# Down-projection regrouped: 4 plain chunks and five Strassen groups with sums in DRAM, three products of a pair added in PSUM, a 48-row projection in widths 512 and 128

## The chip, the cores and the metric

The kernel runs on one core of a Trainium2 chip. The metric is the device time of one execution in microseconds. The engines are TensorE (PE in the profile, its weight loads PEld), VectorE (DVE), ScalarE (ACT), GpSimd (POOL) and SyncE (SP), which here only issues DMAs.

## The reference

One layer of a streaming encoder for 512 prompt frames and 8 x 16 sample frames, 640 token columns in all, with a model width of 2048: a modulated norm, one input projection (its 16 columns for decay and beta are the "48-row projection"), a gated delta rule and a windowed attention, an output projection, and the feed-forward part that the change is about:

```python
x = x + gate1 * (jnp.concatenate([o_d, o_a], axis=-1) @ w_o)
h2 = rms_norm(x, norm2_w) * (1 + scale2) + shift2
u = h2 @ w_up                        # 2048 -> 2 * 5632
u_ext = jnp.concatenate([ffn_prev, u], axis=1)
u_c = causal_dwconv(u_ext, ffn_conv_w) + ffn_conv_b
gt, up = jnp.split(u_c, 2, axis=-1)
x = x + gate2 * ((jax.nn.silu(gt) * up) @ w_down)      # 5632 -> 2048
```

## The kernel before

Activations lie with features on the 128 partitions and the 640 token columns along the free axis, in two halves of 320 (`HALF`): 16 feature chunks for the model width, 44 for the feed-forward width (`NFF`). Every matmul of these projections is done as three in fp32r, high weight by high token part, high by low, low by high. So each weight block of 128 x 512 (a "unit", four chunks) is split on the chip: ACT casts it (`whi`), DVE subtracts (`wlo`). Units come in a fixed stream that `build_stream` writes down; `next_unit` keeps four of them ahead of PE.

The up-projection and part of the down-projection use Strassen's seven products of a 2 x 2 block problem. A product needs a weight operand that is one block or the sum of two (`wsum`, on DVE or POOL), a token operand that is likewise one quarter or a sum of two (`msum`), split in two parts as well, and its result is combined with others afterwards. `product` issues one; `ORDER` = (2, 4, 5, 1, 6, 7, 3) is the order of the seven, each with a PSUM bank of its own.

In the up-projection (`up`, one call for each of 44 pairs) a product has 24 matmuls of 320 columns. Its results are combined into the rows that `conv` then convolves, gates and stores in DRAM (`md`).

The down-projection walks over the 44 chunks in groups, `DGRP` = ((0, 4), (1, 8), (0, 4), (1, 8), (0, 4), (1, 8), (0, 8)). A plain group (0, m) takes m chunks and all 16 output rows, six matmuls for each chunk and row. A split group (1, 8) takes 8 chunks; `down(f)` makes the rows f and f + 8 by seven products of 12 matmuls, 84 in all. `DPOOL` says that of the five weight sums those for products 5, 1 and 7 go to POOL. After each result, `resid` multiplies it by the gate and adds it to `y`, the residual stream, which stays in SBUF through all groups (loaded from `xd`): a scaled add of 256 columns and a product of 64 on DVE, an add of 64 on POOL. `mixes` makes the token operands (`mop`) of a split group from chunks (`mraw`), mostly during the plain group ahead of it; its transfers are issued by POOL.

The order of the instructions on each engine is fixed when the program is built: `Lane`s of background work are stepped between matmuls, as a small model of the engines' clocks permits.

`ab` projects the 16 decay and beta columns, high and low parts in 48 rows of the array, with 64 matmuls of 320 columns.

Of the kernel before, what the change touches and what calls it, by code (L numbers as in the profile page):

```python
# [16 lines left out]
ORDER = (2, 4, 5, 1, 6, 7, 3)  # L17
NF = 8
# [76 lines left out]
class Model:  # L95
    """Estimates when each engine and each tile is free, to order the instructions of parallel tasks."""
# [79 lines left out]
class Ring:  # L176
    """Slots taken in turn, each a tag of a pool."""
# [18 lines left out]
class Slots:  # L196
    """Tiles of any width up to n in the slots of a ring."""
# [30 lines left out]
class Kern:  # L228
# [80 lines left out]
    def build_stream(self):  # L309
# [23 lines left out]
        for i in range(NFF):  # L333
            quarters("u", i, ORDER[4:] if i < NP else ORDER, i < NP)
        n = 0
        for split, m in DGRP:
            for u in range(0 if split else 4 * m):
                self.add_unit(u % 2, (("d", n + u // 2), d["wdn"][n + u // 2]))
            for f in range(8 if split else 0):
                for p in ORDER:  # L340
# [54 lines left out]
    def mm_quarter(self, ps, unit, acts, first, last):  # L395
        nc = self.nc
        hi, lo = unit
        for k, (xh, xl) in enumerate(acts):
            for i, (w, x) in enumerate(((hi, xh), (hi, xl), (lo, xh))):
                nc.tensor.matmul(out=ps, lhsT=w[:, k, :], rhs=x, start=first and k == 0 and i == 0,  # L400
                                 stop=last and k == len(acts) - 1 and i == 2)
# [230 lines left out]
    def ab(self, pool, kp, st):  # L632
        nc, d = self.nc, self.d
        ps, pv = self.main_ps()
# [12 lines left out]
        ps_evac(nc, ps[0:48], a48[:, 0:512].rearrange("p (s c) -> p s c", s=2),  # L647
                a48[:, 512:640].rearrange("p (s b t) -> p s b t", s=2, t=TS))
# [803 lines left out]
    def mix_start(self):  # L1452
        """The last gate and the first block of the output projection, as their operands come."""
# [58 lines left out]
    def head(self, h):  # L1512
        """Convolved queries and keys of head h; calling the result gives them with the values."""
# [28 lines left out]
    def phase2(self):  # L1542
# [4 lines left out]
        self.md = tc.dram_tile([NFF, P, NT], F32, name="md")  # L1547
        self.pd = tc.dram_tile([NP, 4, P, HALF], F32, name="pd")
        with tc.tile_pool(name="xres", bufs=1, reuse_waits="tile") as xr, \
# [20 lines left out]
            with tc.tile_pool(name="opx", bufs=1, reuse_waits="tile") as ox:  # L1570
# [3 lines left out]
                with tc.tile_pool(name="ffn", bufs=1, reuse_waits="tile") as fp:  # L1574
                    self.ffn(Tiles(nc, fp, 1))

    def attn_out(self, pa, load):
        """Output projection with its residual, norm, and the first products of NP pairs."""
# [87 lines left out]
    def operand(self, p, j):  # L1666
        """Token operand of product p for the features of chunks j and j + 8, as a sum of two parts."""
# [34 lines left out]
    def pipe(self, ks, ops, s=0, rB=None):  # L1702
        """Steps that scale rows ks, then make the operands ops, a stage of it a step."""
# [45 lines left out]
    def product(self, p, step=None, nh=2):  # L1749
        ps = self.next_bank()  # L1750
        for h in range(nh):
            un = self.next_unit()
            self.feed(self.rate)
            for k in range(4):
                while len(self.ops[p]) <= 4 * h + k:
                    if self.bg:
                        self.feed()
                    else:
# [3 lines left out]
                self.mm_quarter(ps, (un[0][:, k:k + 1], un[1][:, k:k + 1]), [x], h == 0 and k == 0,  # L1762
                                h == nh - 1 and k == 3)
# [4 lines left out]
    def ffn(self, fp):  # L1768
# [17 lines left out]

        def up(i):
# [8 lines left out]
            e = hs[i] if i < NP else fp.tile([P, HALF], F32, tag="e", name="e")  # L1796
            for q, pr in enumerate(ORDER):
                if i < NP and q < 4:
                    continue
                ps = self.product(pr, lambda: mid(2 * q, t5))  # L1800
                if pr == 2:
                    nc.scalar.copy(out=t2, in_=ps)
                elif pr == 4:
                    p4 = ps
                elif pr == 5:
                    nc.scalar.copy(out=t5, in_=ps)
                    nc.gpsimd.tensor_tensor(out=e, in0=t2, in1=t5, op=ALU.add)
                elif pr == 1:
                    v.tensor_tensor(out=e, in0=ps, in1=e, op=ALU.subtract)
                    step(7)  # L1810
                    ext = [prep(i, n) for n in range(2)]
                    add(v, quad(ext[1], 0), qin(p4), qin(t2))
                elif pr == 6:
                    v.tensor_tensor(out=t2, in0=ps, in1=e, op=ALU.add)
                elif pr == 7:
                    v.tensor_tensor(out=e, in0=ps, in1=e, op=ALU.add)
                    if i < NP:
                        ext = list(short)
                    add(nc.gpsimd, quad(ext[0], 0), quad(ext[1], 0), qin(e))
                elif pr == 3:  # L1820
                    add(v, quad(ext[0], 1), qin(ps), qin(t5))
                    add(nc.gpsimd, quad(ext[1], 1), quad(ext[0], 1), qin(t2))
                step(2 * q + 1)
                if i == NFF - 1 and q == 3:
                    self.lanes["c"].add(chunks())
# [76 lines left out]
        acts, ops, raws, ap, ox = {}, {}, [], self.ap, self.ox  # L1902
        stag = [(ap, f"a{x}{k}") for k in range(6, 16) for x in "hl"] + [(ox, f"ex{k}") for k in range(8)]
        spare = Ring(None, "", 0)
        spare.slots = [[ap, f"a{x}{k}", None] for k in (4, 5) for x in "hl"]
        sums = Slots(spare, NT)

        def raw(c):
            tag = ("ftm", "fext")[len(raws) // 2 % 2]
            raws.append(c)  # L1910
            t = fp.tile([P, 658], F32, tag=tag, name="mraw", bufs=2)[:, 0:NT]
            nc.gpsimd.dma_start(out=t, in_=self.md[c])
            return t

        def whole(c, s, t):
            """Both parts of chunk c, in slot s."""
            tags = [(ap, f"a{x}{s}") for x in "hl"] if s < 4 else stag[2 * s - 8:2 * s - 6]
            hi, lo = (p.tile([P, NT], F32R, tag=n, name=f"m{x}") for x, (p, n) in zip("hl", tags))
            yield (t,)
            nc.scalar.copy(out=hi, in_=t)  # L1920
            yield (hi,)
            v.tensor_tensor(out=lo, in0=t, in1=hi.bitcast(F32), op=ALU.subtract)
            acts[c] = (hi, lo)
            self.done.add(("m", c))

        def mixes(c0, fetch):
            """Token operands of all products for chunks c0 .. c0 + 7, a stage of several at a time."""
            todo, src, hi, low = [(k, q) for k in range(4) for q in range(7)], {}, {}, {}
            for n in range(len(todo) + 3):
                if n < 28:  # L1930
                    k, q = todo[n]
                    if q == 0:
                        while k + 2 > EARLY and self.steps:
                            yield
                        b = [[t[:, s * HALF:(s + 1) * HALF] for s in range(2)] for t in fetch[k]()]
                        (b11, b12), (b21, b22) = b
                        expr = {2: (b11,), 5: (b22,), 4: (b21, b11, ALU.subtract), 1: (b11, b22, ALU.add),
                                6: (b11, b12, ALU.add), 7: (b21, b22, ALU.add), 3: (b12, b22, ALU.subtract)}
                        yield b21, b11
                    x = expr[ORDER[q]]  # L1940
                    src[n] = x[0]
                    if len(x) > 1:
                        src[n] = sums.tile([P, HALF], F32, "", "msum")
                        e = nc.gpsimd if DMIXP[q - 1 - (q > 2)] else v
                        e.tensor_tensor(out=src[n], in0=x[0], in1=x[1], op=x[2])
                if 0 <= n - 1 < 28:
                    k, q = todo[n - 1]
                    yield (src[n - 1],)
                    pool, tag = stag[4 * q + k]
                    t = pool.tile([P, NT], F32R, tag=tag, name="mop")  # L1950
                    hi[n - 1], low[n - 1] = t[:, 0:HALF], t[:, HALF:NT]
                    nc.scalar.copy(out=hi[n - 1], in_=src[n - 1])
                m = n - 2
                if 0 <= m < 28:
                    yield (hi[m],)
                    v.tensor_tensor(out=low[m], in0=src[m], in1=hi[m].bitcast(F32), op=ALU.subtract)
                    ops[c0][ORDER[todo[m][1]]].append((hi[m], low[m]))

        def chunks():
            c0, ts = 0, []  # L1960
            for c in range(4):
                ts.append(ap.tile([P, NT], F32, tag=f"ah{c + 8}", name="mraw"))
                nc.gpsimd.dma_start(out=ts[c], in_=self.md[c])
            for g, (split, m) in enumerate(DGRP):
                if split:
                    ops[c0] = {p: [] for p in ORDER}
                    rs, early = [], EARLY if g == 1 else 0

                    def get(k):
                        if k < early:  # L1970
# [231 lines left out]
```

## Time and profile before

| | |
|---|---|
| timed runs, median of 3 | 3141.67 us (3140.43 to 3145.48) |
| span of the profiled execution | 3137.7 us |
| median of the timed runs less that span | 4.0 us |
| PE busy | 2974.9 us (95%), 19841 matmuls |
| DVE busy | 2319.3 us (74%) |
| ACT busy | 1195.7 us (38%) |
| POOL busy | 1147.2 us (37%) |
| DMA | 428.32 MB |

A row of the table by stages has the stage, its length, then for PE, PEld, DVE, ACT and POOL the busy time and in brackets the number of instructions, then the granted clock of PE, the share of the DMA engines and GB/s. A row of a group of instructions has line, engine, operation, output and inputs, shapes, count, then busy time, mean ns of one, and the idle time of the engine ahead of them with what ended it. A row of the timeline has start, duration, engine and instruction. A row for one tile has the least, middle and largest duration in ns, then the first and last start. Nearly all instructions have the line 90, that of a helper, so they are told apart by the names of their tiles. An engine that waits inside an instruction is shown as busy.

### The profile page before, as it was taken

What the parts mean: (1) busy time and instruction counts of PE and PEld (TensorE: products, weight loads), DVE (VectorE), ACT (ScalarE), POOL (GpSimd) and SP (SyncE); (2) the same over time, 40 slices, a digit from 0 to 9 for tenths busy, and PEclk for the clock granted to TensorE, in tenths of its full rate; (3) what the DMA queues carried; (4) which work ended last, traced back from release to release, by engine and by line L of the source; (5) the groups of instructions that cost most, each with busy time, mean ns of one, the idle gap of its engine ahead of it and who ended that gap; (6) DMA issues with size and microseconds to landing.
All of it is one profiled execution on the core that took longest, in us unless ns stands there. A gap on an engine that the chain in (4) does not pass through costs nothing. (4 is left out here: it accounts for less than half of the span.)

```text
span 3137.7 us, 53459 instructions
## 1 busy us (share of the span) xinstructions
PE 2974.9 (95%) x19841; PEld 2795.6 (89%) x19841; DVE 2319.3 (74%) x4513; ACT 1195.7 (38%) x2245; POOL 1147.2 (37%) x1665
## 2 busy tenths in 40 slices
PE   6999999999999999987999999999999988999898
PEld 2688889899999978876899999999999988989898
DVE  4333437778886424798889899889999899999962
ACT  2432334333442312553444444444444433333321
POOL 2210013233422311465333333333333466666631
PEclk8999989999999999999999999999999999999999
DMA  8755533222223788546433333333333532323232
GB/s 339 283 182 182 176 116 85 78 75 90 79 80 114 254 296 293 165 148 207 140 110 99 96 101 102 102 106 96 101 101 97 176 136 81 115 81 111 90 102 74
DMA packets 189988, 428.32 MB, mean 137 GB/s; under 512 B 49778, under 2 KB 77968, under 8 KB 189712
## 3 DMA queue, kind: packets, MB, share of 16 engines
q1 hardware_dynamic: 152000, 362.15, 35.1%
q0 software_dynamic: 14960, 51.51, 4.8%
q10 hardware_dynamic: 22768, 11.25, 1.4%
q8 instruction: 156, 2.56, 0.3%
q14 instruction: 104, 0.85, 0.1%
HBM read 381.70 MB, written 44.96 MB: 136 GB/s over the span
## 5 line engine op out<-in xcount | busy, mean ns | idle before, releaser
L90 DVE TENSOR_TENSOR wlo<-raw,whi 128x512 fp32r<-128x512 f32 x576 | 446.0, 779 | 317.7 <-ACT whi L90 290.9
L90 ACT CAST whi<-raw 128x512 fp32r<-128x512 f32 x576 | 353.1, 619 | 526.5 <-PE mm L90 361.0
L90 ACT CAST whi<-wsum 128x512 fp32r<-128x512 f32 x560 | 342.4, 619 | 348.0 <-PE mm L90 102.2
L90 DVE TENSOR_TENSOR wlo<-wsum,whi 128x512 fp32r<-128x512 f32 x560 | 435.8, 779 | 22.1 <-ACT whi L90 19.3
L90 PE MATMUL mm<-mh,wlo 128*128 128x320 f32 x1536 | 431.8, 312 | 10.0 <-DVE wlo L90 9.9
L90 PE MATMUL mm<-mh,whi 128*128 128x320 f32 x1536 | 431.2, 311 | 8.2 <-DVE qsq L90 6.6
L90 PE MATMUL mm<-ml,whi 128*128 128x320 f32 x1536 | 430.1, 310 | 0.0
L90 DVE TENSOR_TENSOR wsum<-raw 128x512 f32<-128x512 f32 x463 | 369.1, 797 | 81.9 <-DMA raw<-in_wup 77.8
L90 PE MATMUL mm<-hh,wlo 128*128 128x320 f32 x1376 | 330.6, 322 | 7.6 <-DVE wlo L90 7.6
L90 PE MATMUL mm<-hh,whi 128*128 128x320 f32 x1376 | 327.5, 319 | 4.6 <-ACT hh L90 3.2
L90 PE MATMUL mm<-hl,whi 128*128 128x320 f32 x1376 | 327.0, 319 | 0.6 <-DVE hl L90 0.6
L90 PEld LDWEIGHTS mm<-mh,wlo 128*128 128x128 f32 x1536 | 277.0, 188 | 23.9 <-DVE wlo L90 12.1
L90 PE MATMUL mmd<-mh,wlo 128*128 128x320 f32 x1024 | 292.1, 311 | 6.1 <-DVE wlo L90 6.1
L90 PEld LDWEIGHTS mm<-mh,whi 128*128 128x128 f32 x1536 | 277.6, 188 | 19.0 <-issue 7.1
L90 PE MATMUL mmd<-ml,whi 128*128 128x320 f32 x1024 | 292.0, 310 | 2.4 <-DVE ml L90 2.3
L90 PE MATMUL mmd<-mh,whi 128*128 128x320 f32 x1024 | 292.1, 311 | 0.5 <-ACT qacc L90 0.5
L90 PEld LDWEIGHTS mm<-ml,whi 128*128 128x128 f32 x1536 | 277.4, 189 | 6.9 <-issue 6.7
L90 PEld LDWEIGHTS mm<-hh,wlo 128*128 128x128 f32 x1376 | 230.7, 191 | 21.2 <-issue 11.0
L90 PEld LDWEIGHTS mm<-hh,whi 128*128 128x128 f32 x1376 | 230.1, 191 | 21.7 <-issue 12.8
L90 PEld LDWEIGHTS mm<-hl,whi 128*128 128x128 f32 x1376 | 230.2, 190 | 19.6 <-issue 16.5
L90 POOL TENSOR_TENSOR y<-y,rst 128x64 f32<-128x64 f32 x224 | 122.2, 545 | 208.5 <-DVE rst L90 206.0
L90 PEld LDWEIGHTS mmd<-mh,wlo 128*128 128x128 f32 x1024 | 186.7, 189 | 7.7 <-DVE wlo L90 7.7
(426 smaller groups left out, 6491.7 us busy)
## 6 DMA issues: line engine op xcount, KB each, us to landing
raw<-in_wup SPq DMA_DIRECT2D x206, 512.0 KB, 3.7
araw<-in_adaw SPq DMA_DIRECT2D x256, 256.0 KB, 5.1
raw<-in_wdn SPq DMA_DIRECT2D x88, 512.0 KB, 3.5
raw<-in_win SPq DMA_DIRECT2D x82, 512.0 KB, 3.7
araw<-in_adaw SPq DMA_DIRECT2D x64, 512.0 KB, 6.4
raw<-in_wo SPq DMA_DIRECT2D x48, 512.0 KB, 5.7
mraw<-md POOLq DMA_DIRECT2D x44, 320.0 KB, 4.6
md<-ftm SPq DMA_DIRECT2D x44, 256.0 KB, 5.3
```

The source lines that it names most:

```text
L90: return f(*args, **kw)
```

## The change

The down-projection becomes one plain group of 4 chunks and five split groups of 8. It has its own function and pool (`down`, `fill`), after the up-projection. The plain group's results are written to DRAM (`yd`) without gate or residual. For each job n (rows f and f + 8 of a group) the sums so far are loaded from `yd`, the group's results are added and the sums are stored again; in the last group the gate and the residual (from `xd`) follow, and the output is stored. All these transfers, and the `stg` pairs of chunks from which `fill` makes the token operands (`dop`), are issued by SP.

The products are issued in the order `CHAIN` = (2, 5, 1, 4, 3, 7, 6). Products 4, 3 and 6 are accumulated by PE onto the banks of 2, 5 and 1 (`ONTO`), after ACT has copied the first results out; what has to be taken off again is subtracted by POOL and DVE. The same holds for the pairs 5 to 43 of the up-projection. Of the weight sums only that of product 7 stays on POOL. `ab` uses widths 512 and 128 in place of two of 320. Doc strings go as well.

```diff
+CHAIN = (2, 5, 1, 4, 3, 7, 6)
+ONTO = {4: 2, 3: 5, 6: 1}
...
-DGRP = ((0, 4), (1, 8), (0, 4), (1, 8), (0, 4), (1, 8), (0, 8))
-EARLY = 2
-DPOOL = {2: 0, 5: 1, 1: 1, 6: 0, 7: 1}
-DMIXP = (0, 1, 1, 0, 1)
+DGRP = ((0, 4),) + ((1, 8),) * 5
+DPOOL = {2: 0, 5: 0, 1: 0, 6: 0, 7: 1}
...
-                for s in range(2):
-                    nc.tensor.matmul(out=pv[s][0:48], lhsT=st[:, k, :],
-                                     rhs=self.h[k][i][:, s * HALF:(s + 1) * HALF],
+                for s, w in enumerate((512, 128)):
+                    nc.tensor.matmul(out=ps[0:48, s, 0:w], lhsT=st[:, k, :], rhs=self.h[k][i][:, 512 * s:512 * s + w],
                                      start=k == 0 and i == 0, stop=k == KC - 1 and i == 1)
...
+    def chained(self, p, banks, nh, step=None):
+        ps = banks[p] if p in banks else banks[ONTO[p]]
+        return self.product(p, step, nh, ps, p not in ONTO)
+
+    def banks(self):
+        a, b = self.main_ps2(0)[0], self.main_ps2(1)[0]
+        return {2: a[:, 0, 0:HALF], 5: a[:, 1, 0:HALF], 7: b[:, 0, 0:HALF], 1: b[:, 1, 0:HALF]}, a, b
...
+            for q, pr in enumerate(CHAIN):
+                ps = self.chained(pr, banks, 2, lambda: step(2 * q))
                 if pr == 2:
                     nc.scalar.copy(out=t2, in_=ps)
...
                 elif pr == 5:
                     nc.scalar.copy(out=t5, in_=ps)
-                    nc.gpsimd.tensor_tensor(out=e, in0=t2, in1=t5, op=ALU.add)
+                    nc.gpsimd.tensor_tensor(out=t2, in0=t2, in1=t5, op=ALU.add)
                 elif pr == 1:
-                    v.tensor_tensor(out=e, in0=ps, in1=e, op=ALU.subtract)
+                    m1 = fp.tile([P, HALF], F32, tag="t5", name="m1")
+                    nc.scalar.copy(out=m1, in_=ps)
+                    nc.gpsimd.tensor_tensor(out=e, in0=m1, in1=t2, op=ALU.subtract)
+                elif pr == 4:
                     step(7)
                     ext = [prep(i, n) for n in range(2)]
-                    add(v, quad(ext[1], 0), qin(p4), qin(t2))
+                    take(quad(ext[1], 0), qin(ps))
...
+    def fill(self, dp, c0, key):
...
+        def fetch(r, s, d):
+            t = dp.tile([P, 2, HALF], F32, tag="stg", name="stg", bufs=4)
+            k = c0 + 4 * r + 2 * d
+            nc.sync.dma_start(out=t, in_=self.mdt[k:k + 2, :, s * HALF:(s + 1) * HALF].rearrange("k p c -> p k c"))
+            return t
...
+            if len(t) > 1:
+                nc.gpsimd.tensor_tensor(out=t[0], in0=t[0], in1=t[1], op=e[2])
...
+            for i in range(2):
+                v.tensor_tensor(out=tl[2 + i], in0=t[:, i], in1=tl[i].bitcast(F32), op=ALU.subtract)
...
+            for q, pr in enumerate(CHAIN):
+                ps = self.chained(pr, banks, 1)
...
+                if pr == 2:
+                    nc.scalar.mul(out=t2, in_=ps, mul=-1.0)
+                elif pr == 5:
+                    nc.scalar.mul(out=t5, in_=ps, mul=-1.0)
+                    nc.gpsimd.tensor_tensor(out=ge[:, 1], in0=t2, in1=t5, op=ALU.add)
+                elif pr == 1:
+                    nc.scalar.copy(out=m1, in_=ps)
+                    nc.gpsimd.tensor_tensor(out=ge[:, 0], in0=m1, in1=ge[:, 1], op=ALU.add)
+                elif pr == 4:
+                    nc.gpsimd.tensor_tensor(out=YA, in0=YA, in1=ge, op=ALU.add)
+                elif pr == 3:
+                    nc.scalar.copy(out=cc, in_=A[:, :, 0:HALF])
+                    v.tensor_tensor(out=YB, in0=YB, in1=A[:, :, 0:HALF], op=ALU.add)
+                    nc.gpsimd.tensor_tensor(out=YA, in0=YA, in1=cc, op=ALU.add)
+                elif pr == 6:
+                    v.tensor_tensor(out=YA, in0=YA, in1=B[:, :, 0:HALF], op=ALU.add)
+                if q == 1:
+                    tail()
+                if q == 3 and n + 1 < njobs:
+                    ys[n + 1] = load(n + 1)
```

On DVE, a job of a split group before, less its residuals (`e`, `c`, `t` are results that read PSUM):

```order
L90 TENSOR_TENSOR wsum<-raw 128x512
L90 TENSOR_TENSOR wlo<-wsum,whi 128x512
L90 TENSOR_TENSOR wlo<-raw,whi 128x512
L90 TENSOR_TENSOR e<-mm_32902,e 128x320
L90 TENSOR_TENSOR c_32958<-mm_32902,t_32877 128x320
L90 TENSOR_TENSOR wlo<-wsum,whi 128x512
L90 TENSOR_TENSOR t_32877<-mmd,e 128x320
L90 SCALAR_TENSOR_TENSOR y_0_27778<-c_32958,mod,y_0_27778 128x256
L90 TENSOR_TENSOR rst<-c_32958,mod 128x64
L90 TENSOR_TENSOR wlo<-raw,whi 128x512
L90 TENSOR_TENSOR e<-mm_32984,e 128x320
```

And the same part of a job now:

```order
L90 TENSOR_TENSOR wlo<-raw,whi 128x512
L90 TENSOR_TENSOR dop<-stg,dop 128x320 x2
L90 TENSOR_TENSOR wsum<-raw 128x512
L90 TENSOR_TENSOR wlo<-wsum,whi 128x512
L90 TENSOR_TENSOR wsum<-raw 128x512
L90 TENSOR_TENSOR wlo<-wsum,whi 128x512
L90 TENSOR_TENSOR dop<-stg,dop 128x320 x2
L90 TENSOR_TENSOR wsum<-raw 128x512
L90 TENSOR_TENSOR wlo<-wsum,whi 128x512
L90 TENSOR_TENSOR y_29642<-y_29642,mmd 128x640
L90 TENSOR_TENSOR wlo<-wsum,whi 128x512 x2
L90 TENSOR_TENSOR y_29641<-y_29641,mm_29705 128x640
```

A sum of weights now stands before most splits, the splits of the next group's operands (`dop`) lie among them, and two adds from PSUM of 640 columns are left of the results.

On POOL, a job of a split group before:

```order
L90 TENSOR_TENSOR wsum<-raw 128x512
L90 TENSOR_TENSOR e<-t_33037,t_33038 128x320
L90 TENSOR_TENSOR wsum<-raw 128x512
L90 TENSOR_TENSOR y_0_27831<-y_0_27831,rst 128x64
L90 TENSOR_TENSOR wsum<-raw 128x512
L90 TENSOR_TENSOR e<-e,c_33118 128x320
L90 TENSOR_TENSOR t_33037<-t_33037,t_33038 128x320
L90 TENSOR_TENSOR y_0_27433<-y_0_27433,rst 128x64
L90 TENSOR_TENSOR y_1_27434<-y_1_27434,rst 128x64
L90 TENSOR_TENSOR y_1_27832<-y_1_27832,rst 128x64
```

And now:

```order
L90 TENSOR_TENSOR stg<-stg 128x640
L90 TENSOR_TENSOR wsum<-raw 128x512
L90 TENSOR_TENSOR stg<-stg 128x640
L90 TENSOR_TENSOR ge<-t_29706,t_29707 128x320
L90 TENSOR_TENSOR ge<-t_29708,ge 128x320
L90 TENSOR_TENSOR y_29641<-y_29641,ge 128x640
L90 TENSOR_TENSOR y_29641<-y_29641,cc 128x640
```

Ten instructions a job have become five, and one or two sums of `stg` in the jobs in which a fill runs; four of these are 640 columns wide.

## Rows read from the trace of the kernel before

**Rows 1.** Busy time by stages: up-projection, first plain, second split, last plain group.
```profile
1600.00:2400.00 800.00, 800.00 (x5457) 800.00 (x5456) 724.09 (x1200) 371.61 (x618) 272.68 (x443) 1.00 0.32 100
2484.00:2541.00 57.00, 56.40 (x385) 56.14 (x384) 49.23 (x110) 21.50 (x42) 37.80 (x60) 1.00 0.68 234
2723.00:2840.00 117.00, 104.81 (x673) 101.19 (x672) 112.57 (x177) 41.58 (x76) 77.50 (x79) 0.97 0.24 79
3014.00:3127.00 113.00, 112.22 (x766) 111.95 (x765) 43.18 (x100) 20.47 (x33) 18.02 (x35) 1.00 0.29 94
```
**Rows 2.** Timeline of PE: first plain product, first split product, last product.
```profile
2484.33 0.46 PE L90 MATMUL mmd<-mh,whi 128*128 128x320 f32 x2
...
2541.51 0.46 PE L90 MATMUL mmd<-mop,whi 128*128 128x320 f32 x2
...
3127.29 0.46 PE L90 MATMUL mm<-mh,wlo 128*128 128x320 f32 x2
```
**Rows 3.** Groups of instructions of DVE, 2723 to 2840 us.
```profile
L90 DVE TENSOR_TENSOR wlo<-wsum,whi 128x512 fp32r<-128x512 f32 x39 | 40.5, 1038 | 3.7 <-ACT whi L90 3.6
L90 DVE TENSOR_TENSOR wsum<-raw 128x512 f32<-128x512 f32 x15 | 17.0, 1135 | 0.0
L90 DVE TENSOR_TENSOR wlo<-raw,whi 128x512 fp32r<-128x512 f32 x18 | 16.6, 924 | 0.3 <-ACT whi L90 0.2
L90 DVE SCALAR_TENSOR_TENSOR y<-t,mod,y 128x256 f32<-128x256 f32 x14 | 6.6, 473 | 0.0
L90 DVE TENSOR_TENSOR rst<-e,mod 128x64 f32<-128x64 f32 x7 | 6.3, 893 | 0.0
L90 DVE TENSOR_TENSOR ml<-mraw,mh 128x640 fp32r<-128x640 f32 x4 | 5.2, 1289 | 0.0
...
L90 DVE TENSOR_TENSOR e<-mmd,e 128x320 f32<-128x320 f32 x8 | 3.8, 481 | 0.1
```
**Rows 4.** Groups of instructions of POOL, 2723 to 2840 us.
```profile
L90 POOL TENSOR_TENSOR wsum<-raw 128x512 f32<-128x512 f32 x22 | 31.7, 1440 | 0.0
L90 POOL TENSOR_TENSOR y<-y,rst 128x64 f32<-128x64 f32 x32 | 19.2, 601 | 22.1 <-DVE rst L90 22.1
L90 POOL TENSOR_TENSOR e<-e,c 128x320 f32<-128x320 f32 x8 | 10.6, 1328 | 0.5 <-DVE e L90 0.5
L90 POOL TENSOR_TENSOR e<-t,t 128x320 f32<-128x320 f32 x8 | 9.8, 1219 | 10.0 <-ACT t L90 10.0
L90 POOL TENSOR_TENSOR t<-t,t 128x320 f32<-128x320 f32 x7 | 7.3, 1048 | 7.2 <-DVE t L90 7.2
```
**Rows 5.** Timeline of DVE and POOL inside that split group.
```profile
2761.32 0.68 DVE L90 TENSOR_TENSOR wlo<-wsum,whi 128x512 fp32r<-128x512 f32 x1
2761.36 1.37 POOL L90 TENSOR_TENSOR e<-t,t 128x320 f32<-128x320 f32 x1 [1.12 <-ACT t L90]
...
2761.92 1.37 DVE L90 TENSOR_TENSOR wlo<-raw,whi 128x512 fp32r<-128x512 f32 x1
2762.70 1.73 POOL L90 TENSOR_TENSOR wsum<-raw 128x512 f32<-128x512 f32 x1
2763.21 0.48 DVE L90 TENSOR_TENSOR e<-mm,e 128x320 f32<-128x320 f32 x1
...
2763.61 0.48 DVE L90 TENSOR_TENSOR c<-mm,t 128x320 f32<-128x320 f32 x1
2764.01 0.97 DVE L90 TENSOR_TENSOR wlo<-wsum,whi 128x512 fp32r<-128x512 f32 x1
```
**Rows 6.** Single tiles: POOL's 640-column add, a 512-column add of DVE from PSUM.
```profile
L90 POOL TENSOR_TENSOR ss_acc<-ss_acc,sq x7: 1527/2049/2055, 8.7 to 26.8; 128x640 f32<-128x640 f32 x7
...
L90 DVE TENSOR_TENSOR S<-S,pu x16: 670/686/689, 572.0 to 1017.0; 128x512 f32<-128x512 f32 x16
```
**Rows 7.** The tile of the 48-row projection's weights.
```profile
L90 PE MATMUL mm<-hh,ab_st x32: 302/308/391, 161.4 to 173.7; 128*48 128x320 f32 x32
```
**Rows 8.** Timeline of SP in the first plain group.
```profile
2507.22 1.80 SPq L90 DMA_DIRECT2D y<-xd  x4
```

More of the change, by code (lines that the diff above doesn't have):

```diff
@@ L1575, in phase2 @@
                     self.ffn(Tiles(nc, fp, 1))
+                with tc.tile_pool(name="dn", bufs=1, reuse_waits="tile") as dp:
+                    self.down(Tiles(nc, dp, 1))
     def attn_out(self, pa, load):
@@ L1785, in add, with take @@
                 eng.tensor_tensor(out=o, in0=x, in1=y, op=ALU.add)
+        def take(o, x):
+            for o, x in zip(o, x):
+                nc.scalar.copy(out=o, in_=x)
         def up(i):
@@ L1795, in up @@
             t2, t5 = (fp.tile([P, HALF], F32, tag=n, name=n) for n in ("t2", "t5"))
[L1796 to L1800, printed above, removed]
+            if i < NP:
+                e = hs[i]
+                for q, pr in enumerate(ORDER):
+                    if q < 4:
+                        continue
+                    ps = self.product(pr, lambda: mid(2 * q, t5))
+                    if pr == 6:
+                        v.tensor_tensor(out=t2, in0=ps, in1=e, op=ALU.add)
+                    elif pr == 7:
+                        v.tensor_tensor(out=e, in0=ps, in1=e, op=ALU.add)
+                        ext = list(short)
+                        add(nc.gpsimd, quad(ext[0], 0), quad(ext[1], 0), qin(e))
+                    else:
+                        add(v, quad(ext[0], 1), qin(ps), qin(t5))
+                        add(nc.gpsimd, quad(ext[1], 1), quad(ext[0], 1), qin(t2))
+                    step(2 * q + 1)
+                conv(i, ext)
+                return
@@ L1823, in up @@
                 step(2 * q + 1)
-                if i == NFF - 1 and q == 3:
-                    self.lanes["c"].add(chunks())
+                if i == NFF - 1 and q == 1:
+                    self.lanes["c"].add(first_chunks())
             conv(i, ext)
@@ L1915, in whole @@
[L1915 to L1970, printed above, removed]
-                            rs.append([stag[18 - 4 * k + j][0].tile([P, NT], F32, tag=stag[18 - 4 * k + j][1], name="mraw")
-                                       for j in range(2)])
-                            for j in range(2):
-                                nc.gpsimd.dma_start(out=rs[k][j], in_=self.md[c0 + k + 4 * j])
-                        else:
-                            rs.append((raw(c0 + k), raw(c0 + k + 4)))
-                    for k in range(max(1, early)):
-                        get(k)
-                    def fetch(k):
-                        while len(rs) < min(k + 2, 4):
-                            get(len(rs))
-                        return rs[k]
-                    while g > 1 and ("g", g - 2) not in self.done:
-                        yield
-                    yield from mixes(c0, [lambda k=k: fetch(k) for k in range(4)])
-                else:
-                    if g:
-                        ts = [raw(c0 + s) for s in range(4)]
-                    for s in range(m):
-                        while g > 1 and ("g", g - 2 + s // 4) not in self.done:
-                            yield
-                        yield from whole(c0 + s, s, ts[s])
-                        if s + 4 < m:
-                            ts.append(raw(c0 + s + 4))
-                c0 += m
@@ new lines, in ffn, with first_chunks @@
+        ap = self.ap
+        self.acts, raws = {}, {}
+        def first_chunks():
+            n = DGRP[0][1]
+            for c in range(n):
+                raws[c] = ap.tile([P, NT], F32, tag=f"ah{n + c}", name="mraw")
+                nc.sync.dma_start(out=raws[c], in_=self.md[c])
+            for c in range(n):
+                hi, lo = (ap.tile([P, NT], F32R, tag=f"a{x}{c}", name=f"m{x}") for x in "hl")
+                yield (raws[c],)
+                nc.scalar.copy(out=hi, in_=raws[c])
+                yield (hi,)
+                v.tensor_tensor(out=lo, in0=raws[c], in1=hi.bitcast(F32), op=ALU.subtract)
+                self.acts[c] = (hi, lo)
+                self.done.add(("m", c))
@@ new lines, in ffn @@
+        while self.steps:
+            self.steps.pop(0)[1]()
+    def fill(self, dp, c0, key):
+        nc, v = self.nc, self.nc.vector
+        todo, src = [(p, d) for p in CHAIN for d in range(2)], {}
+        expr = {2: ((0, 0),), 5: ((1, 1),), 1: ((0, 0), (1, 1), ALU.add), 4: ((1, 0), (0, 0), ALU.subtract),
+                3: ((0, 1), (1, 1), ALU.subtract), 7: ((1, 0), (1, 1), ALU.add), 6: ((0, 0), (0, 1), ALU.add)}
+        self.dops[key] = ops = {p: [] for p in CHAIN}
+        def fetch(r, s, d):
[3 more added lines that the diff above has]
+            return t
+        n = len(todo)
+        for m in range(-1, n):
+            if m + 1 < n:
+                p, d = todo[m + 1]
+                src[m + 1] = [fetch(r, s, d) for r, s in expr[p][:2]]
+            if m < 0:
+                continue
+            t, e = src.pop(m), expr[todo[m][0]]
+            yield tuple(t)
+            if len(t) > 1:
+                nc.gpsimd.tensor_tensor(out=t[0], in0=t[0], in1=t[1], op=e[2])
+            t = t[0]
+            slot, user = self.slots.pop(0)
+            while user is not None and user not in self.done:
+                yield
+            self.slots.append((slot, ("p", key, todo[m][0])))
+            tl = [pool.tile([P, NT if len(slot) == 2 else HALF], F32R, tag=tag, name="dop") for pool, tag in slot]
+            yield (t,)
+            if len(slot) == 2:
+                nc.scalar.copy(out=tl[0].rearrange("p (k c) -> p k c", k=2), in_=t)
+                tl = [x[:, i * HALF:(i + 1) * HALF] for x in tl for i in range(2)]
+            else:
+                for i in range(2):
+                    nc.scalar.copy(out=tl[i], in_=t[:, i])
+            yield tuple(tl[:2])
+            for i in range(2):
+                v.tensor_tensor(out=tl[2 + i], in0=t[:, i], in1=tl[i].bitcast(F32), op=ALU.subtract)
+                ops[todo[m][0]].append((tl[i], tl[2 + i]))
```

175 lines of the change are left out of this document (88 added, 87 removed).

## Prediction

> **What bounds the kernel now.** I read the table by stages first, then the groups of instructions of VectorE (DVE) and GpSimd (POOL) in one split group, then the timeline of a few microseconds inside it. In the up-projection TensorE (PE) is busy for 800 of 800 us and passes 5457 matmuls, 0.1466 us each [rows 1]; it is the bound there, with DVE at 724 and POOL at 273. The plain groups of the down-projection are the same picture: 56.4 of 57 us, 112.2 of the last group's 113 before its tail [rows 1]. The split groups are different: 117 us for 672 matmuls, which PE alone would pass in 98.5 (672 x 0.1466), while DVE is busy for 112.6 of the 117 [rows 1]. So in three stretches of the whole program DVE, not PE, sets the time, and the change makes five such stretches out of three.
>
> Why DVE is full there is the point on which everything rests. A split `wlo` of 512 columns takes 0.68 us undisturbed, the next instruction starting 0.60 after it; a 320-column add that reads PSUM has its next one 0.40 later [rows 5]. But in the split group `wlo<-wsum` takes 1.04 on the mean, `wlo<-raw` 0.92, `wsum` 1.14 [rows 3]. The timeline shows why. POOL's 320-column add starts at 2761.36, behind the `wlo` of 2761.32; the next `wlo`, at 2761.92, then takes 1.37, 0.69 more than its own 0.68, and ends just after the add. In turn POOL's 512-column sum of 2762.70 is released at 2763.21, when that `wlo` lets go. The two PSUM adds of 2763.21 and 2763.61 run beside it at their 0.48, and the `wlo` of 2764.01 pays 0.29 [rows 5]. So an instruction of DVE with two tensors in SBUF and a POOL add with two tensors in SBUF don't run together: one waits for the other's end, and an add that reads PSUM is free of it. I call the time for which POOL so keeps DVE out its hold: 0.69 us for 320 columns, 2763.21 to 2764.30 = 1.09 for 512, and on that slope (2.1 ns a column) 1.36 for 640 and 0.15 for 64. POOL has an add of two full 640-column tensors elsewhere, 1.53 at its shortest [rows 6], which fits.
>
> The Trainium skill says the same in SBUF — State Buffer, section Who interferes with whom: a VectorE instruction with two SBUF inputs contends with a GpSimd instruction that reads SBUF, since its second input comes through the read interface that both share. This case's trace agrees, with the 0.69 us above. It speaks against a change that gives DVE more such instructions and POOL wider ones.
>
> How much of the holds DVE really pays is read from the means. Over the 117 us: `wlo<-wsum` 39 x (1.038 - 0.68) = 14.0, `wlo<-raw` 18 x 0.24 = 4.4, `wsum` 15 x 0.455 = 6.8, `rst<-e` 7 x 0.68 = 4.8, `ml` 4 x 0.48 = 1.9 (0.81 undisturbed, by the columns): 31.9 us [rows 3]. POOL's holds in it are 22 x 1.09 + 23 x 0.69 + 32 x 0.15 = 44.7 [rows 4]. DVE pays 0.71 of them; the rest falls beside its adds from PSUM and its scaled adds, which never lengthen [rows 3]. Without the payment DVE would be busy for 112.6 - 31.9 = 80.7 us, 10.1 a job (a job is the seven products of rows f and f + 8), of which about 39 x 0.40 and 31 x 0.39, 35%, are such free instructions [rows 3].
>
> **The change, part by part.**
>
> *PE.* Of the 44 chunks 4 are plain where 20 were, and five split groups stand where three did. Matmuls: 1920 + 3 x 672 = 3936 before, 384 + 5 x 672 = 3744 after; 192 x 0.1466 = 28 us less PE work. It counts only where PE sets the pace: the 16 plain chunks that go cost 16 x 14.1 = 225 us at PE's pace, the two split groups that come cost whatever DVE needs.
>
> *DVE in a job.* Seven `wlo` and four `wsum` (two before, since only product 7 stays on POOL): 11 x 0.60 = 6.60. The new `dop` splits, 28 per group: 3.5 x 0.40 = 1.40. Two 640-column adds from PSUM in place of five of 320 and four residuals: 2 x 0.73 = 1.46 (a 512-column add of that kind takes 0.69 at most [rows 6], next 0.60 later, plus 128 columns at 1.04 ns). Together 9.46, against 10.1. Two-tensor SBUF work is now 8.00 of it, 85%, against 65%.
>
> *POOL's holds in a job.* One `wsum` 1.09, two `ge` 2 x 0.69, two adds into `y` 2 x 1.36, ten `stg` sums per group 1.25 x 1.36: 6.89 us. Before: 44.7 / 8 = 5.6. Fewer instructions, but the removed ones were mostly the 64-column kind.
>
> *The job.* If holds and two-tensor instructions exclude each other and every other instruction of DVE hides under a hold, the floor is 8.00 + 6.89 = 14.9 us, a payment of 0.79 of the holds. If the payment grows with the share of two-tensor work, 0.71 x 0.85 / 0.65 = 0.93, the job is 15.9. I take 0.85, between the two: 9.46 + 0.85 x 6.89 = 15.3. PE needs 84 x 0.1466 = 12.3 of it, so it waits. At the old payment of 0.71 the job would be 14.35; I keep this as the low end. Before, a job took 14.6.
>
> *Last group.* No fill, but four residuals: DVE 6.60 + 1.46 + 4 x 0.39 + 4 x 0.25 = 10.6, holds 1.09 + 1.38 + 2.72 + 0.60 = 5.8; 10.6 + 0.85 x 5.8 = 15.5 a job.
>
> *Plain group.* 2484.33 to 2541.51, 57.2 us [rows 2], kept: 384 matmuls. DVE has 16 `wlo`, the first fill's 28 `dop`, 9.6 + 11.2, and 13.6 of holds, all under PE's 56; uncovered it would be the 34 us of its sum, still less.
>
> *Tail.* 3137.7 - 3127.3 = 10.4 before [rows 2]; now a 0.8 add and two residuals from SBUF instead of PSUM, and four output transfers at the end instead of two: 11.8.
>
> *Up-projection.* In a pair DVE loses a 0.40 subtraction and, by their columns, adds of 2 x 0.33 and 2 x 0.13; ACT gains one copy for the subtraction and four for these adds, and POOL one 320-column subtraction (hold 0.69). PE is at 800 of 800, so I count 0 for the gain. If this cover went, a pair (168 matmuls, 24.6 us) would need DVE's 22.3 (724 / 800 of it) less about 1.3 plus 0.7: still under 24.6.
>
> *DMA.* SP now issues per job two weight blocks, four `y` loads, four stores and on the mean three `stg` fetches, 13 x 0.45 = 5.9 us of 15 (four `y` loads took 1.80 [rows 8]). Bytes: 1.05 + 1.31 + 0.98 = 3.3 MB in 15.3 us, 218 GB/s; the first plain group already moved 234 [rows 1]. The `y` loads are issued a job ahead, and a `y` load is queued behind the store that frees its tile; what stands behind them on SP is the next `stg` fetch, for which POOL, then ACT and DVE would wait. I count 0, and 1.2 us a job if each of the mean 1.25 two-block fetches came a microsecond late (rival 3).
>
> *48-row projection.* 64 matmuls of 320 columns become 32 of 512 and 32 of 128, the same columns: 0. If each 128-column one still took a 320-column one's place, 32 x 0.6 x 0.1466 = 2.8 us, against a stretch of 12 us [rows 7]. POOL, DVE and ACT behind it have nothing else new.
>
> *Sum*, against the profiled execution's span, 3137.7: before, from the first plain product, 653.4. After: 57.2 + 8 x (4 x 15.3 + 15.5) + 11.8 = 57.2 + 613.6 + 11.8 = 682.6, that is 29 us more. The timed runs' median lies 4.0 above the span, and I carry that over: 3141.7 + 29 = **3171 us**. The ends: payment 0.71, 8 x (4 x 14.35 + 14.7) = 577, 646 in all, 3134; payment 0.93, 8 x (4 x 15.9 + 16.0) = 637, 706, 3194.
>
> **The rivals.**
> 1. *PE becomes the bound (faster).* The chained products halve the PSUM reads, and PE has two jobs' banks in place of little more than one. If DVE's job came under 12.3 us, the split groups would take 98.5 each: 57.2 + 492.5 + 11.8 = 561.5, 92 less, 3050. For it: DVE's own 9.46 leaves 2.8 us for holds. Against it: 6.89 us of them, so DVE would have to pay under 0.41, where it pays 0.71 now. It decides at a payment of 0.41. Chance 0.10.
> 2. *DVE pays no more than now.* POOL's wide adds come just when DVE adds from PSUM, or while it waits for ACT: 0.71 or a little less, 3134 (3115 to 3148). For it: the two PSUM adds are 0.82 long, so one hides more of a hold. Against it: the floor of 14.9. Chance 0.20.
> 3. *Every hold is paid, or fetches come late on top.* 9.46 + 6.89 = 16.35 a job, 16.4 in the last group: 654 + 69 = 723, 3211; a late fetch of 1.2 us at payment 0.85 gives 3209 as well. By the exclusive lock that the Trainium skill states there (SBUF — State Buffer, Who interferes with whom) this is what DVE would see with nothing to hide a hold under. For it: DVE has a two-tensor instruction next nearly always. Against it: the PSUM adds. Chance 0.12.
> 4. *The forecast,* payment 0.75 to 0.95, 3148 to 3197. Chance 0.58.
>
> That the products don't chain in PSUM is no rival: the order of PE's instructions has them so.
>
> **How the numbers follow.** About 0.2% (6 us) is what a measurement of this kernel can tell from no change. Faster by more: rival 1 and three fifths of rival 2, 0.22. Within: the rest of rival 2 and the edge of the forecast, 0.10. Slower: 0.68. The range leaves out rival 1 and the worst of rival 3: 3115 to 3207. The forecast's own range is 3148 to 3197.
>
> **What would show it.** Right: split groups of 122 to 126 us, DVE busy above 95% in them, `wlo<-wsum` with a mean above 1.1 us, PE waiting for `wlo` and no longer for DVE's sums; the up-projection unchanged with PE full. Wrong: `wlo` near 0.7 and PE full in the split groups (rival 1), or long waits of POOL and ACT for `stg` and `y` transfers (rival 3). The prediction fails if 640-column adds of POOL hold DVE for much less than 1.36 us, or if DVE finds other work during them.

## The result, and the profile after

The changed kernel takes 3509.2 us (3503.2 to 3513.6) against 3142.6: a ratio of 1.117 (95% interval 1.115 to 1.119), 367 us slower. The forecast was 3171, its range ended at 3207, and even the worst rival stood at 3211. The sign was right; most of the time went where the prediction had counted nothing.

The stages of the changed kernel, with the columns of [rows 1] (the up-projection, the plain group, one split group without its neighbours, and a stretch of 3.6 us that is spoken of below):

```profile
1600.00:2400.00 800.00, 680.79 (x4221) 661.79 (x4220) 545.15 (x803) 316.69 (x603) 212.86 (x363) 0.94 0.24 78
2766.00:2823.00 57.00, 57.00 (x391) 57.00 (x390) 29.66 (x46) 26.98 (x44) 11.42 (x13) 1.00 0.73 244
3102.00:3232.00 130.00, 107.76 (x673) 101.86 (x674) 126.56 (x134) 56.79 (x106) 76.81 (x50) 0.97 0.63 204
2023.60:2027.20 3.60, 3.60 (x16) 3.60 (x15) 1.56 (x3) 0.72 (x2) 0.00 (x0) 0.53 0.59 130
```

The first row is the surprise. In the same 800 us of the up-projection PE passes 4221 matmuls where it passed 5457 [rows 1], and DVE is less busy than before, 545 against 724. So no engine is full. A pair of 168 matmuls takes 168 x 800 / 4221 = 31.8 us, not 24.6; 7.2 us over 39 chained pairs are 281 us. The plain group is as forecast, and a split group takes 130 us, where 122 to 126 had been named.

What PE waits for in that stretch (engine, tile and what it waits for; us in total, times, longest):

```profile
PE mmd L90 <- ACT fext L90: 55.5, 25, 2.2
PE mm L90 <- DVE e L90: 49.8, 25, 4.1
PE mmd L90 <- ACT t L90: 14.0, 25, 0.6
```

Each of the three comes once a pair; before, PE waited for nothing there. The timeline of PE, and below it that of ACT, around one of the long ones:

```profile
2020.70 0.31 PE L90 MATMUL mmd<-mh,wlo 128*128 128x320 f32 x1
2023.24 0.56 PE L90 MATMUL mmd<-op,whi 128*128 128x320 f32 x2 [2.23 <-ACT fext L90]
2023.64 0.32 PE L90 MATMUL mmd<-op,wlo 128*128 128x320 f32 x1
...
2022.06 0.75 ACT L90 ACTIVATE ftm<-ftm 128x656 f32<-128x656 f32 x1 [2.30 <-DVE ftm L90]
2022.72 0.47 ACT L90 COPY fext<-mmd 128x256 f32<-128x256 f32 x2
```

At 2020.70 the last matmul of product 4 starts (its operands are `mh`). Product 3 (`op`) is next. It adds to the bank of product 5, whose result ACT had copied out while product 1 ran, so nothing in that bank is in the way. Yet it starts only when ACT has copied the result of product 4 out of the neighbouring bank, and that copy stood in ACT's queue behind a SiLU that waited for DVE. The two banks are halves of one tile `mmd`. After the wait PE's granted clock is 0.53 for 3.6 us (the stage row above), its 1.2 GHz level: 0.27 us a matmul. The three waits sum to 119.3 us in 800, the loss is (5457 - 4221) x 0.1466 = 181. For the other 62 PE is busy: it takes 680.8 us for matmuls that at the pace of before take 618.8. Most of that is the slower clock, by its mean of 0.94 some 0.06 x 800 = 48 us; what the rest is, no row shows.

### The profile page after: what moved, and what is told of

Its sections match the earlier page's. It is cut to its first block, busy times and chain, and to the rows that moved or that the text cites. A ratio compares the mean times of both kernels' runs of the same rounds, so it can differ in the third digit from the quotient of the medians.

```text
span 3501.3 us, 53647 instructions
## 1 busy us (share of the span) xinstructions
PE 3069.6 (88%) x19649; PEld 2843.1 (81%) x19649; DVE 2413.5 (69%) x4070; ACT 1335.9 (38%) x2613; POOL 1186.7 (34%) x1532
## 5 line engine op out<-in xcount | busy, mean ns | idle before, releaser
L90 DVE TENSOR_TENSOR wlo<-wsum,whi 128x512 fp32r<-128x512 f32 x640 | 568.8, 894 | 141.6 <-ACT whi L90 140.3
L90 DVE TENSOR_TENSOR wsum<-raw 128x512 f32<-128x512 f32 x575 | 456.4, 794 | 152.7 <-DMA raw<-in_wup 109.6
L90 PE MATMUL mmd<-dop,whi 128*128 128x320 f32 x1280 | 297.7, 320 | 36.8 <-ACT t L90 36.8
L90 PE MATMUL mm<-ex,whi 128*128 128x320 f32 x664 | 216.9, 327 | 80.2 <-DVE e L90 76.8
L90 PE MATMUL mm<-mh,whi 128*128 128x320 f32 x968 | 277.0, 313 | 10.7 <-DVE qsq L90 8.1
L90 PE MATMUL mm<-mh,wlo 128*128 128x320 f32 x968 | 277.4, 313 | 9.8 <-DVE wlo L90 9.7
L90 PE MATMUL mmd<-op,whi 128*128 128x320 f32 x712 | 202.7, 372 | 89.5 <-ACT fext L90 86.7
L90 PE MATMUL mm<-ml,whi 128*128 128x320 f32 x968 | 275.9, 312 | 0.3 <-DVE ml L90 0.3
L90 PEld LDWEIGHTS mmd<-dop,whi 128*128 128x128 f32 x1280 | 221.1, 195 | 48.4 <-ACT t L90 48.4
L90 PEld LDWEIGHTS mmd<-op,whi 128*128 128x128 f32 x712 | 151.5, 239 | 100.0 <-ACT fext L90 96.9
```

The lines of the kernel that those rows point to most:

```text
L90: return f(*args, **kw)
```

## The experiments

**Which part of the change.** One kernel has the change with the up-projection of before, one the kernel before with only the chained pairs of the up-projection:

```diff
-            quarters("u", i, ORDER[4:] if i < NP else CHAIN, i < NP)
+            quarters("u", i, ORDER[4:] if i < NP else ORDER, i < NP)
...
-            for q, pr in enumerate(CHAIN):
+            for q, pr in enumerate(ORDER):
...
```

> The changed kernel with the up-projection of before (seven banks, no sums in PSUM); the down-projection stays changed. Theory A: the up-projection passes its matmuls as before, so the time shows what the new down-projection alone costs: 3509 - 289 = 3220 us, 78 above before, where the prediction had 29. Rival D (the up-projection is slowed by something else that the new kernel does beside it, such as the order of the weights for the down-projection or memory): it stays slow, above 3400.

> The kernel before with only the chained pairs of the up-projection; its down-projection stays. Theory A: 3142 + 289 = 3431 us (3415 to 3445). Rival D: well under 3431, since the cause lies in the rest of the change.

Measured: 3226.0 and 3431.3 us (one run each), beside 3145.1 of the kernel before. The up-projection costs 283 to 286 us and the rest of the change 78 to 81, together the 367. Rival D falls: each part costs nearly the same without the other.

**Is it the tile?** Each bank of a chained pair in a PSUM tile of its own (a tile of two banks, of which one is used):

```diff
-            banks = self.banks()[0]
+            t4 = [self.main_ps2(n)[1][0] for n in (0, 1, 0, 1)]
+            banks = dict(zip((2, 5, 1, 7), t4))
```

> The changed kernel, but each of the four banks of a chained pair of the up-projection lies in a PSUM tile of its own; the sums in PSUM and the order of the products stay. Theory A (a product that is written into one half of a two-bank tile waits until the other half's result is read out, because both halves count as one tile): the waits for ACT's copies and for DVE's e, 29.9 us in 200, go, and with them the 16.3 us of slow clock behind them; 39 pairs give back 7.4 us each, 289 us: 3220 us (3200 to 3245), TensorE full between 2000 and 2200 us. Rival B (the added product truly waits, for the copy of the first result out of its own bank): nothing changes, 3500 or more. Rival C (the low clock is a cause of its own and not a result of the waits): only the waits go, 39 x 4.8 = 187 us: about 3320.

> The kernel before with the chained pairs of the up-projection, each bank in a tile of its own. Theory A: TensorE sets the pace of the up-projection as before, so nothing is left to gain or lose there: 3142 us, within 6. Rival B: 3431 or more, as with two-bank tiles.

Measured: 3341.6 (ratio 1.0625, 1.060 to 1.065) and 3255.9 us (1.035, 1.033 to 1.037). All three waits are gone, 168 to 175 us came back, and B falls; but A promised 289 and, in the second kernel, all of it. By its time alone the first kernel lies nearest to C's 3320. The rows speak against C: what is left is one other wait, about once a pair, and the granted clock is 0.98 where it was 0.94. Of the (4861 - 4221) x 0.1466 = 94 us regained in the 800, 54 are waits (119.3 less the 65.0 of the new one), so some 40 are not; the clock, 0.04 x 800 = 32 us, is most of these. The up-projection of the first of these kernels, and what PE waits for in it:

```profile
1600.00:2400.00 800.00, 734.86 (x4861) 724.75 (x4860) 637.64 (x927) 356.23 (x696) 262.30 (x419) 0.98 0.28 90
...
PE mmd L90 <- DVE wlo L90: 65.0, 33, 2.7
```

To see the tile's effect without any sum in PSUM, I gave the kernel before the same neighbourhood: successive products in the two halves of one tile.

```diff
-        if n < 2:
-            self.btile = [None, None] if n == 0 else self.btile
-            self.btile[n] = self.main_ps2(n)[0]
-        return self.btile[n % 2][:, n // 2, 0:HALF]
+        if n % 2 == 0:
+            self.btile = self.main_ps2(n // 2)[0]
+        return self.btile[:, n % 2, 0:HALF]
```

> The kernel before with one edit: successive products of the up-projection and of the split groups take the two banks of one PSUM tile, and then the two of the next tile, instead of alternating between two tiles; nothing is added up in PSUM. Theory A: three or four times a pair a product waits for the read of its neighbour, 0.6 us behind a copy of ACT and 1.3 behind an add of DVE, with slow clock behind it: 4 to 6 us a pair in the up-projection, 3142 + 39 x 5 = 3340 (3270 to 3420). Rival B (only the sum in one bank waits): no change, 3142.

Measured: 3353.4 us (one run), 211 more than before. From the first split product to the last (`mop`) it takes 517.6 us where it took 470.3, so 47 of the 211 arise in the split groups, which the edit reaches too. Its waits in 1600 to 2400 us, where it passes 4715 matmuls, less 19.0 us for ACT's `whi` and 10.4 for DVE's `fext`:

```profile
PE mm L90 <- DVE e L90: 14.3, 7, 2.1
PE mmd L90 <- DVE e L90: 14.3, 7, 2.1
...
PE mmd L90 <- ACT t L90: 7.6, 14, 0.6
PE mm L90 <- ACT t L90: 7.6, 14, 0.6
```

So the wait needs no sum: a product written into one half of a two-bank tile waits for the read of the other half. Whether the chip asks for that, or only the semaphores that the program is built with, no run here shows. The old rotation alternated between tiles, which put a whole product, 3.5 us, between a read and the next write to its tile.

**The rest of the up-projection.** In the four-tile kernel the timeline of SP, DVE and PE shows what is late:

```profile
2072.00 1.77 SPq L90 DMA_DIRECT2D raw<-in_wup  x4
...
2076.77 0.69 DVE L90 TENSOR_TENSOR wsum<-raw 128x512 f32<-128x512 f32 x1 [3.60 <-DMA raw<-in_wup]
2077.38 0.68 DVE L90 TENSOR_TENSOR wlo<-wsum,whi 128x512 fp32r<-128x512 f32 x1
2078.12 0.41 PE L90 MATMUL mmd<-ex,wlo 128*128 128x320 f32 x1 [1.78 <-DVE wlo L90]
```

and the same queue of the kernel before:

```profile
2049.84 12.41 SPq L90 DMA_DIRECT2D raw<-in_wup  x4
```

Before, the four loads of a pair were spread over 12.4 us; now they go out together, and DVE waits for one with a `wlo` behind it that PE needs. The five slots for raw blocks are taken in turn. The block loaded first is read by products 2 and 6, and in the new order 6 comes last, so that slot holds up all that follow. One edit exchanges 6 and 7:

```diff
+UCHAIN = (2, 5, 1, 4, 3, 6, 7)
...
-            for q, pr in enumerate(CHAIN):
+            for q, pr in enumerate(UCHAIN):
```

> The four-tile up-projection with products 6 and 7 of the chained pairs exchanged; the down-projection as in the change. Theory E (the weights come late: the five slots of raw weights are taken in the order in which blocks are first used, the oldest block of a pair is still needed by product 6, which comes last, and so the next pair's second block is fetched only then; DVE waits 3.6 us for it with a wlo for TensorE queued behind): the next fetch comes one product, 3.5 us, sooner, the wait of 2.1 us and the slow clock behind it, 3 us a pair, go: 3226 us as with the unchained up-projection (3215 to 3240). Rival F (DVE simply has too much queued ahead of that wlo): 3342, no change.

> The same up-projection before the old down-projection. Theory E: TensorE full in the up-projection, 3142 us within 6, and nothing gained, as TensorE is the bound there. Rival F: 3256.

Measured: 3232.9 (one run) and 3156.1 us (ratio 1.004, 1.0025 to 1.0055). Theory E holds and F falls; 109 and 100 us came back. In the first of these kernels the loads of a pair go out over some 5 us, and little is left of the wait:

```profile
2063.75 4.67 SPq L91 DMA_DIRECT2D raw<-in_wup  x4
...
PE mmd L91 <- DVE wlo L91: 7.1, 5, 1.9
```

Some 7 to 14 us stay, where E had promised none in the second kernel: PE passes 5387 matmuls in the 800 us, not 5457, which is 10 us, and 7.1 of them are what is left of this wait.

**The down-projection.** Is DVE full because of GpSimd's holds? All adds of the job, the chunk sums and the weight sum of product 7 go from GpSimd to DVE in the new down-projection, behind the up-projection of before. In a second kernel the weight sums and the 320-column adds of the split groups of before go the same way; their 64-column adds stay.

```diff
-DPOOL = {2: 0, 5: 0, 1: 0, 6: 0, 7: 1}
+DPOOL = {2: 0, 5: 0, 1: 0, 6: 0, 7: 0}
...
-                    nc.gpsimd.tensor_tensor(out=YA, in0=YA, in1=ge, op=ALU.add)
+                    v.tensor_tensor(out=YA, in0=YA, in1=ge, op=ALU.add)
...
```

> The new down-projection behind the unchained up-projection, with the weight sum of product 7, the sums of chunks and the four adds of a job moved from GpSimd to DVE. Theory H (a two-tensor add of GpSimd keeps DVE's two-tensor instructions out for longer than DVE itself would take for the same add): a job of DVE's own 9.46 becomes 9.46 + 0.60 + 0.80 + 1.50 + 0.94 = 13.3 us with no holds, against 15.0 with them, and with the 1.1 us of idle time 14.4 against 16.2: 40 x 1.8 = 72 us less than 3226: 3154 (3135 to 3175), wlo near 0.68 in the mean. Rival G (holds are not what fills DVE, its count of instructions is): DVE takes over 3.8 us of work a job, 3226 + 100 or more.

> The kernel before with all weight sums and the three 320-column adds of its split groups moved from GpSimd to DVE. Theory H: a split group of DVE's undisturbed 80.7 us plus 22 x 0.60 plus 23 x 0.40 plus 3.4 for the 64-column adds left on GpSimd and 4.4 idle is 111 us against 117: three groups, 18 us less, 3124 (3115 to 3135). Rival G: DVE is given 22 us more in each group, 3142 + 60 = 3200 or more.

Measured: 3145.3 (ratio 1.001, 1.000 to 1.002; 81 less than with GpSimd) and 3113.3 us (0.9907, 0.989 to 0.992). Rival G falls: giving DVE more instructions made both kernels faster. Groups of DVE in a split group of the changed kernel:

```profile
L90 DVE TENSOR_TENSOR wlo<-wsum,whi 128x512 fp32r<-128x512 f32 x41 | 45.7, 1129 | 2.8 <-ACT whi L90 2.8
L90 DVE TENSOR_TENSOR wsum<-raw 128x512 f32<-128x512 f32 x33 | 33.9, 1026 | 0.3
L90 DVE TENSOR_TENSOR dop<-stg,dop 128x320 fp32r<-128x320 f32 x28 | 30.4, 1123 | 0.0
L90 DVE TENSOR_TENSOR wlo<-raw,whi 128x512 fp32r<-128x512 f32 x16 | 12.2, 764 | 0.3 <-ACT whi L90 0.3
```

and of the kernel with the adds on DVE (2782 to 2895 us, one split group):

```profile
L90 DVE TENSOR_TENSOR wlo<-wsum,whi 128x512 fp32r<-128x512 f32 x41 | 28.2, 701 | 0.0
L90 DVE TENSOR_TENSOR wsum<-raw 128x512 f32<-128x512 f32 x40 | 28.1, 702 | 0.0
L90 DVE TENSOR_TENSOR dop<-stg,dop 128x320 fp32r<-128x320 f32 x30 | 13.5, 496 | 0.0
...
L90 DVE TENSOR_TENSOR y<-y,ge 128x640 f32<-128x640 f32 x9 | 7.5, 834 | 0.0
```

The same 41 splits take 1129 ns and 701; before the change it was 1038 [rows 3]. A GpSimd add of 640 columns held DVE for 1.36 us by the prediction's reckoning, while DVE does that add itself in 0.83. In the same split group of the changed kernel a `wlo` beside such an add pays just that, 2.03 - 0.68 = 1.35:

```profile
3214.25 1.88 POOL L90 TENSOR_TENSOR y<-y,cc 128x640 f32<-128x640 f32 x1
...
3214.64 2.03 DVE L90 TENSOR_TENSOR wlo<-wsum,whi 128x512 fp32r<-128x512 f32 x1
```

Do the tiles matter here as well? Four tiles in the down-projection, with the adds left on GpSimd (the two adds of 640 columns become four of 320):

```diff
-            banks, A, B = self.banks()
+            t4 = [self.main_ps2(k)[1][0] for k in (0, 1, 0, 1)]
+            banks = dict(zip((2, 5, 1, 7), t4))
```

> The unchained up-projection and the new down-projection with the adds left on GpSimd, each bank of a job in a tile of its own. If DVE under the holds sets these jobs (theory H), the 1.4 us a job that TensorE waits for ACT's t are mostly time that it would wait for wlo anyway: 3226 to 3210. If the tiles set them (theory A alone), 40 x 1.4 and the slow clock behind it go: 3150.

Measured: 3216.0 us (one run), 10 less, which is no more than runs of one kernel differ by (3138.0 to 3149.3 for the kernel before): under the holds the tiles hardly count, as expected of theory H.

**What the runs point to.** Adds on DVE, four tiles, and the residual's rows (`xo`) loaded at the start of a job, behind the up-projection of before; and then the whole change with these and the two edits of the up-projection:

```diff
+            if last:
+                x = [dp.tile([P, 2, HALF], F32, tag="stg", name="xo", bufs=4) for _ in range(2)]
...
-                if q == 3 and last:
-                    x = [dp.tile([P, 2, HALF], F32, tag="stg", name="xo", bufs=4) for _ in range(2)]
```

> The unchained up-projection and the new down-projection with its adds on DVE, and two edits more: each bank of a job in a PSUM tile of its own, and in the last group the rows of the residual are loaded at the start of a job instead of behind its fourth product. By theory A the waits for ACT's t (0.53 a job) and the slow clock behind them go, and 35 jobs of 13.1 us become 12.4 (84 x 0.1466 = 12.3 for TensorE): 25 us; DVE waits 20 us in the last group for those rows, and its 126 us become about 100: 3145 - 50 = 3095 us (3080 to 3115). If the jobs of 13.1 are DVE's own 13.3 us and not TensorE's waits, only the last group gains: 3120.

> The whole change, chained pairs of the up-projection included, with all that the runs have pointed to: a tile for each bank in both projections, product 6 ahead of 7 in the up-projection, the adds of the down-projection on DVE, the residual's rows loaded early. If the causes add up and nothing else is left, it is the 3108 us of the same down-projection behind the unchained up-projection plus the 11 that the chained pairs still cost over it: 3119 (3110 to 3130), faster than before by 0.7%. If a further cost of the chained up-projection hides in the whole, 3142 or more.

Measured: 3107.6 (ratio 0.9887, 0.987 to 0.991) and 3119.1 us (0.992, 0.990 to 0.994). Both are faster than the kernel before, by 1.1% and 0.8%. The first has the lowest time, but the kernel before with its adds on DVE, at 3113.3, is within 0.2% of it. What the first gained over 3145.3 lies in the last group, where seven jobs from `cc` to `cc` take 96.5 us against 126.1; a middle group takes 110.6 against 112.2, so most of the 25 us that theory A promised for the middle groups did not come. The causes add up: mended, the whole change is 390 us faster than as it was written.

## Why the prediction was wrong

**The step that failed: "PE is at 800 of 800, so I count 0 for the gain."** The up-projection was put at nothing and cost 283 to 286 us. The check beside it, that a pair without this cover would need DVE's 22.3 us less about 1.3 plus 0.7 and so stay under 24.6, did not help: a pair took 31.8. The step added up the work of engines and asked which was full. It did not ask of each product which tile it writes and what must be read there first. Each of the products 5, 3 and 6 follows directly on one in the same tile; the read between them, by ACT or DVE and behind other work in their queues, then lies on PE's path. This cost some 170 us. The reordered products also changed when weight blocks come free, which the same step passed over: 100 to 109 us more. With the 7 to 14 that stay, that is the 283 to 286 of the 367. The names `mmd` and `mm` in the order of PE's instructions held the first cause, and the list of blocks that each product reads the second.

**"PE has two jobs' banks in place of little more than one" (rival 1)** counted banks. Tiles count: two of a job's four banks can't be read and written side by side. The Trainium skill says in PSUM — Partial Sum Buffer, section Summary: rules for kernel authors, that while matmuls run one reads from another bank. Product 3 kept to that and waited all the same (2.23 us); it was the tile, not the bank, and one bank to a tile took the wait away.

**The job of a split group, 15.3 us: the mechanism was right, the size a little low.** In the group shown (0.68 and 0.48 are what the instructions take undisturbed), the lengthening is 41 x (1.129 - 0.68) + 33 x (1.026 - 0.68) + 16 x (0.764 - 0.68) + 28 x (1.123 - 0.48) = 49.2 us, of holds of 8 x 6.89 = 55.1: a payment of 0.89, forecast 0.85 with 0.93 as its end. With DVE's own 8 x 9.46 = 75.7 us that is 124.9, against 126.6 measured. To it come 3.4 us of idle DVE; the group is 130 us, 16.2 a job. The rule of the Trainium skill (SBUF — State Buffer, section Who interferes with whom) spoke against the change here, and the runs bear it out: 81 us went with the adds moved.

**The last group, 15.5 us a job, was too low by 2.8.** ACT's copy `cc` comes once a job; in the first job of the first split group, of the second and of the last, and in the last job:

```profile
2837.01 0.70 ACT L90 COPY cc<-mmd 128x640 f32<-128x640 f32 x1 [1.24 <-PE mmd L90]
...
2974.45 0.69 ACT L90 COPY cc<-mmd 128x640 f32<-128x640 f32 x1
...
3361.59 0.69 ACT L90 COPY cc<-mmd 128x640 f32<-128x640 f32 x1
...
3489.82 0.70 ACT L90 COPY cc<-mmd 128x640 f32<-128x640 f32 x1 [0.87 <-PE mmd L90]
```

Seven jobs in 128.2 us are 18.3 each; the 24 of the three groups ahead are 16.1. DVE's wait for the residual's rows in these seven jobs (3362 to 3490 us) was

```profile
DVE xo L90 <- DMA xo<-xd: 15.8, 6, 3.6
```

that is 2.3 us a job. The rows were asked for behind the fourth product and needed after the fifth. The prediction counted these loads in no job: the "I count 0" of its paragraph on DMA failed here. With the rows loaded at the start of a job (and the adds on DVE, and four tiles) this wait is gone, and the seven jobs take 96.5 us. Four tiles alone, the adds on GpSimd, left them at 126.7. The prediction's scaled adds that never lengthen hold for [rows 3], not throughout: of the last group's, 0.48 us in the median, the one at 3491.40 took 0.88 beside a GpSimd add of 640 columns.

**Terms that held.** The plain group, 56.3 us from its first product to the next group's (2766.30 to 2822.62) against 57.2; the 48-row projection, whose matmuls begin over 12.4 us (162.8 to 175.2) against 12.3 [rows 7]; and the sign. Of the down-projection, 29 us were forecast and 78 to 81 measured. The difference lies in the jobs: 17.2 us each in the first split group (137.4 us from its `cc` to the next group's), 16.1 in the next three and 18.3 in the last, against 15.3 and 15.5. Why the first group's are longer I did not settle. The tail was shorter than the 11.8 us forecast: 8.3 from the start of the last matmul, at 3492.99.

## What to carry to other kernels

A change in the order of operations changes more than the amounts of work: for each PSUM tile write down who reads it between two writes, in whose queue that read stands, and put a product in between; for each buffer taken in turn, check when the oldest is read last. A sum of busy times only tells what a stage can't be faster than. Before an engine is relieved by another, compare what the relief takes from it: here 0.83 us of VectorE's own time against a hold of 1.35.

## What the runs showed that I had not expected

A wait can cost PE more than its length: behind the 2.23 us at 2023.24 the clock is 0.53 for 3.6 us, and in the up-projection the slower clock made up some 48 of 181 lost us. It does not follow each time. Behind the 2.24 us of the same wait at 1612.31 the clock stayed at 1.00:

```profile
1612.60:1616.20 3.60, 3.60 (x26) 3.60 (x26) 1.63 (x3) 0.87 (x3) 0.00 (x0) 1.00 0.56 132
```

What decides it, no run here shows. A wait of 0.56 us in the same kernel had no such stretch behind it either (the clock is 1.00 from 2010.20 to 2013.80):

```profile
2010.19 0.41 PE L90 MATMUL mmd<-mh,whi 128*128 128x320 f32 x1 [0.56 <-ACT t L90]
2010.44 0.30 PE L90 MATMUL mmd<-ml,whi 128*128 128x320 f32 x1
2010.58 0.31 PE L90 MATMUL mmd<-mh,wlo 128*128 128x320 f32 x1
```

And moving GpSimd's adds to a VectorE that was already busy for 112.6 of 117 us [rows 1] made the kernel before 0.9% faster, more than the 0.6% that the hold had led me to expect.
